# Attention's query projection moved behind the last value stream, and the latents' chunk matrices moved up behind the context's

## The chip, the cores and the metric

The kernel runs on one core of one Trainium2 chip. The metric is the device time of one execution in microseconds (us), the median of three runs. Inputs, weights and output are fp32 in the chip's memory; every projection reads its weights from there once.

## The reference, cut to what matters

The network has two layers on 256 latent tokens (and, in layer 0, 256 context tokens), width 2048. Layer 0 mixes tokens in two ways at once: eight heads of a bidirectional gated delta rule (GDN), and eight heads of attention. The change lies wholly in that mixer.

```python
def gated_delta_chunked(q, k, v, g, beta, s0):      # chunks of 64 tokens
    ...
    m = jnp.where(i[:, None] > i[None, :], jnp.einsum('bhnid,bhnjd->bhnij', kb, k) * decay, 0.0)
    t_inv = lax.linalg.triangular_solve(eye + m, ...)
    ...
    s_fin, o = lax.scan(step, s0, tuple(xs))         # state runs from chunk to chunk

def even_mixer(h, hc, ...):
    pc = hc @ w_in[:, ...]                           # context: keys and values alone
    o_c, s_ctx_fin = gdn_bidirectional(...)          # context first
    ka, va, kb, vb, a, b, qa, qb, za = split_segments(h @ w_in, EVEN_SEGS)
    ...
    o_l, _ = gdn_bidirectional(to_bhtd(q_l), ..., s_ctx_fin)   # latents start from the context's state
    y_gdn = gdn_out_norm(o_l, za, gdn_norm)
    y_na = neighbourhood_attention(heads(qb), heads(kb), heads(vb), k_ctx_na, v_ctx_na, rpb)
    y = jnp.concatenate([y_gdn, y_na], axis=-1) @ w_out
```

Behind the mixer come a SwiGLU feed-forward, layer 1 (a short convolution mixer) and a second feed-forward.

## The kernel before

**Projections.** A weight tile of 512 KB is loaded (`raw`, four rooms), split by ScalarE into a rounded half `whi` and by VectorE into the remainder `wlo` (L175, L246), and TensorE multiplies three products of halves (hi·hi, hi·lo, lo·hi). `fm_stream` (L344) gives features by tokens, `tm_stream` (L299, L300, L304 and, for the last weight tiles, L316) tokens by features; both yield once for each of 16 slices of the input width. The segments of `ev_w_in` are named KA, VA, QA (GDN's keys, values, queries), KB, VB, QB (attention's) and ZA (GDN's gate). QB is needed for the latents alone, so its matmuls are 256 columns wide; those of KB and VB are 512 wide.

**Side work.** `drive` runs a stream step by step. Where it is given `pump`, it lets so many adaLN jobs run for each step (`R_QB`, `R_KB`, `R_ZA`, `R_WO`): one job loads 256 KB of `ada_w` (`araw`) and adds a scaled copy to `acc` on VectorE (L434). Where `counts` is set, it counts steps and, at the steps in `P_INV`, runs the entries of `plan`.

**GDN.** `chunk_matrices(seq)` (seq 1 is the context, 0 the latents) builds the decayed key products `nt`, writes their parts out, and solves the 32 by 32 diagonal blocks by substitution on VectorE (62 small operations, L1018 and L1020). `inverses` assembles the inverse of four heads (a quad) from 32 to 128 by small matmuls on TensorE (L1074, L1081, L1087). `scan` runs the state over two chunks of two directions: for the latents each of the four rounds of a quad is a chain of L1112 and L1121 (state times keys, times queries), L1115 (`R`, VectorE), L1132 (inverse times `R`), L1136 and L1150 (ScalarE), L1140 and L1145 (the state's update) and L1154 (the output's second part).

**Attention.** For each head, `na_scores` loads the keys `kb`, the queries `qb` and a table of biases `bq` (L1289, rows of 256 bytes), adds the mask to the table on VectorE (L1292), multiplies (L1296, L1297) and takes the softmax (L1301 to L1305); `na_values` transposes the weights (L194) and multiplies by the values `vb` (L1320).

**Order in the program.** The context's chunk matrices are made first; QA and VA follow. Then come, counted as steps 1 to 96: two QB streams (32 steps; the result goes to `qb_d` in memory), KB, VB, KB, VB (64 steps; to `kb_d`, `vb_d`). At steps 30 and 32 the context's two quads are inverted; at step 32 the latents' chunk matrices and the context's scan follow; at steps 82 and 84 the latents' quads are inverted and scanned. After the streams come the eight heads of attention, ZA, the GDN heads' output norm, and the output projection W_out, whose first four slices are attention's heads 0 to 3 (`YO`).

This order is not what the engines run. A scheduler places each instruction by a simulated timeline, so work of neighbouring parts is interleaved on each engine's queue; each engine then runs its queue in that order. SyncE (SP) issues nearly all DMAs, one after the other, and an issue waits there until its buffer is free.

## Time and profile before

| | |
|---|---|
| runs | 2732.53 us median (2730.55 to 2732.67) |
| profiled execution | 2736.99 us |
| its span, first to last instruction | 2735.2 us |
| TensorE busy / VectorE / ScalarE / GpSimd | 97% / 70% / 47% / 2% of the span |
| mean granted TensorE clock | 0.991 |

A row of a window gives a stretch of the span, its length, then for each engine the busy time and the number of instructions in it, the granted TensorE clock as a share of full speed, the DMA engines' busy share and the rate in GB/s. PE is TensorE's matmuls, PEld its weight loads, DVE VectorE, ACT ScalarE, POOL GpSimd. A matmul of fp32 operands that were not rounded is two records. The records of matmuls overlap: one of 512 columns lasts about 0.39 us, and in a dense stretch the next starts after 0.23 us.

### The profile page before, as it was taken

To read this page: it belongs to the slowest core of one execution; us is meant where nothing else is said; L and a number is where in the kernel's file an instruction comes from. 1 tells how busy PE (TensorE), PEld (TensorE's weight loads), DVE (VectorE), ACT (ScalarE), POOL (GpSimd) and SP (SyncE) were. 2 spreads that over 40 slices of the span, in tenths; PEclk is the share of its full clock that TensorE was granted. 3 is DMA by queue.
4 is the path that set the end of the run, shared out by engine and by line. 5 is a ranking of instruction groups with operands and counts; after the bars stand their busy time and mean duration, and the time that the engine had idled before them with its cause. 6 is when DMAs were issued, how large, how long until landed. Compare 5 with 4: busy or idle time off the path is not lost.

```text
span 2735.2 us, 37578 instructions
## 1 busy us (share of the span) xinstructions
PE 2660.5 (97%) x13775; PEld 2188.8 (80%) x13775; DVE 1921.6 (70%) x2640; ACT 1276.9 (47%) x1849; POOL 56.7 (2%) x85
## 2 busy tenths in 40 slices
PE   6999999998989999999999999999999999999998
PEld 4688898886768888888888878888878888888886
DVE  4378796886658877766778878888575555545675
ACT  3257633323544544444455555444464444445554
POOL 0000100110000000000000000000000000000000
PEclk9999999998999999999999999999999999999999
DMA  9955598797737888888888859998567777656553
GB/s 368 347 156 181 167 315 259 271 342 216 234 108 258 290 287 293 299 292 277 291 284 288 297 157 336 324 337 280 184 225 235 226 238 226 219 188 220 195 194 112
DMA packets 286852, 684.80 MB, mean 250 GB/s; under 512 B 57161, under 2 KB 99761, under 8 KB 285259
## 3 DMA queue, kind: packets, MB, share of 16 engines
q1 hardware_dynamic: 280388, 669.26, 72.8%
q10 hardware_dynamic: 4375, 9.48, 1.0%
q0 software_dynamic: 1904, 3.67, 0.4%
q8 instruction: 108, 1.77, 0.2%
q14 instruction: 77, 0.63, 0.1%
HBM read 659.21 MB, written 23.10 MB: 249 GB/s over the span
## 4 chain that ended last, share of the span: by engine, by line
PE 88%; DMA 5%; DVE 3%; ACT 2%; SPq 1%; issue 1%; DVEq 0%; ACTq 0%
PE mm L299 21%; PE mm L304 21%; PE mm L300 21%; PE mm L344 10%; PE mm L316 8%; DMA araw<-in_ada_w_dram 2%; PE sm L194 2%; PE sm L595 1%; PE gd L344 1%; DMA bq<-in_ev_rpb_dram 1%; DMA raw<-in_ev_w_in_dram 1%; PE gd L938 1%; DVE wlo L246 0%; DMA xn<-in_ctx_dram 0%; SPq L1010 0%
## 5 line engine op out<-in xcount | busy, mean ns | idle before, releaser
L246 DVE TENSOR_TENSOR wlo<-raw,whi 128x1024 fp32r<-128x1024 f32 x800 | 971.9, 1222 | 457.9 <-ACT whi L175 444.4
L175 ACT ACTIVATE whi<-raw 128x1024 fp32r<-128x1024 f32 x800 | 843.5, 1062 | 886.8 <-PE mm L304 617.6
L299 PE MATMUL mm<-whi,fhi 128*128 128x512 f32 x1232 | 482.0, 393 | 2.6 <-DVE fhi L1437 2.6
L300 PE MATMUL mm<-wlo,fhi 128*128 128x512 f32 x1232 | 479.7, 390 | 0.5 <-DVE wlo L246 0.5
L304 PE MATMUL mm<-whi,flo 128*128 128x512 f32 x1232 | 389.9, 390 | 0.0
L399 DVE SCALAR_TENSOR_TENSOR acc<-araw,cT,acc 128x1024 f32<-128x1024 f32 x224 | 286.5, 1279 | 36.2 <-DMA araw<-in_ada_w_dram 32.9
L344 PE MATMUL mm<-hB,whi 128*128 128x512 f32 (+1 forms) x1064 | 273.5, 348 | 1.0 <-DVE hB L619 1.0
L299 PEld LDWEIGHTS mm<-whi,fhi 128*128 128x128 f32 x1232 | 231.3, 188 | 50.9 <-DVE fhi L1437 4.0
L304 PEld LDWEIGHTS mm<-whi,flo 128*128 128x128 f32 x1232 | 231.1, 188 | 48.4
L300 PEld LDWEIGHTS mm<-wlo,fhi 128*128 128x128 f32 x1232 | 231.2, 188 | 47.6 <-DVE wlo L246 1.2
L299 PE MATMUL mm<-whi,ahi 128*128 128x512 f32 x664 | 259.0, 390 | 0.0
L300 PE MATMUL mm<-wlo,ahi 128*128 128x512 f32 x664 | 258.3, 389 | 0.0
L304 PE MATMUL mm<-whi,alo 128*128 128x512 f32 x664 | 206.6, 389 | 0.0
L344 PEld LDWEIGHTS mm<-hB,whi 128*128 128x128 f32 x1064 | 181.4, 190 | 24.3 <-DVE hB L619 2.2
L344 PE MATMUL mm<-hB,wlo 128*128 128x512 f32 (+1 forms) x532 | 178.0, 347 | 0.6 <-DVE wlo L246 0.6
L434 DVE SCALAR_TENSOR_TENSOR acc<-araw,cT,acc 128x512 f32<-128x512 f32 x192 | 142.7, 746 | 24.8 <-DMA araw<-in_ada_w_dram 23.3
L178 ACT ACTIVATE ahi<-prodT 128x256 fp32r<-128x256 f32 x176 | 73.0, 418 | 182.9 <-PE mm L300 178.1
L304 PEld LDWEIGHTS mm<-whi,alo 128*128 128x128 f32 x664 | 124.6, 188 | 25.9
L300 PEld LDWEIGHTS mm<-wlo,ahi 128*128 128x128 f32 x664 | 124.7, 188 | 25.7
L299 PEld LDWEIGHTS mm<-whi,ahi 128*128 128x128 f32 x664 | 124.6, 188 | 25.7
L299 PE MATMUL mm<-whi,dhi 128*128 128x512 f32 x336 | 131.2, 393 | 1.2 <-DVE dhi L1437 1.2
L300 PE MATMUL mm<-wlo,dhi 128*128 128x512 f32 x336 | 130.8, 390 | 0.0
(410 smaller groups left out, 3413.9 us busy)
## 6 DMA issues: line engine op xcount, KB each, us to landing
araw<-in_ada_w_dram SPq DMA_DIRECT2D x288, 512.0 KB
raw<-in_ffn_w_down_dram SPq DMA_DIRECT2D x176, 512.0 KB
raw<-in_ffn_w_gate_dram SPq DMA_DIRECT2D x160, 512.0 KB
raw<-in_ffn_w_up_dram SPq DMA_DIRECT2D x160, 512.0 KB
raw<-in_ev_w_in_dram SPq DMA_DIRECT2D x112, 512.0 KB
araw<-in_ada_w_dram SPq DMA_DIRECT2D x192, 256.0 KB
raw<-in_od_w_in_dram SPq DMA_DIRECT2D x96, 512.0 KB
raw<-in_ev_w_out_dram SPq DMA_DIRECT2D x32, 512.0 KB
```

The lines of the kernel that those rows point to most:

```text
L175: ACT.activation(dst, src, AF.Copy)
L178: ACT.activation(hi, src, AF.Copy)
L194: return PE.transpose(dst, src, ident[:n, :n])
L246: last_lo[0] = DVE.tensor_tensor(lo, raw, hi, op=OP.subtract).ins
L299: PE.matmul(ps[ti][n], a, hi[:, n * 512:(n + 1) * 512], start=first, stop=False)
L300: ins = PE.matmul(ps[ti][n], a, lo[:, n * 512:(n + 1) * 512], start=False, stop=False).ins
L304: last_mm[0] = PE.matmul(ps[ti][n], b, hi[:, n * 512:(n + 1) * 512], start=False, stop=False).ins
L316: ins = PE.matmul(ps[ti][n], a(t), w[:, c_], start=False, stop=a is ll and hi is group[-1][0]).ins
L344: last_mm[0] = PE.matmul(o, wt, h_(slice(0, len(ws)), mv, k), start=i == 0 and g == 0 and j == 0, stop=i == len(ks) - 1 and g == len(group ...
L399: DVE.scalar_tensor_tensor(acc, raw, cT[:, k:k + 1], acc, op0=OP.mult, op1=OP.add)
L434: DVE.scalar_tensor_tensor(accs[n], raws.pop(i), cT[:, k:k + 1], accs[n], op0=OP.mult, op1=OP.add)
L595: ins = PE.matmul(pr[32 * j:32 * j + 32, :], cT2[:, g + j, :], raw[:, j].rearrange("p s n -> p (s n)"), start=g == 0, stop=g == KT - 4).ins
```

## The change

The two QB streams no longer come first. The first one, `queries(0)`, runs behind the last VB stream and ahead of attention's first scores; the second, `queries(1)`, inside the loop over heads, ahead of head 4's scores. Their results are not sent to memory: three pairs of heads stay in the staging rooms `nst`, the fourth in the room that `qb` had. The counted steps 1 to 64 are now KB, VB, KB, VB, and 65 to 96 the queries.

The latents' chunk matrices move from behind the context's second inverse (step 32) to step 2 (`P_CH`), ahead of both inverses of the context. So that both can be alive, the latents' `n64`, `n32`, `dgs` get rooms of other tiles (`o_t`, `vtok`), and the solve is done in place in `dgs`. The context's quads are inverted at steps 16 and 22, and the second quad's `xd` is loaded after the first inverse, into the same room; the latents' quads are inverted and scanned at steps 50 and 56. Loads of weights in attention, the queries and ZA are given high priority by the scheduler (`urgent`). The clearing of the mixer's `acc` goes from GpSimd to VectorE. Two pump rates change.

```diff
-P_INV = (30, 32, 82, 84)
+P_CH = 2
+P_INV = (16, 22, 50, 56)
...
-R_KB = 1.8
-R_ZA = 1.5
+R_KB = 1.6
+R_ZA = 2.0
...
-            SP.dma_start(raw[:, :, o:o + w], ap.rearrange("(k p) n -> p k n", p=128)[:, k0:k0 + nk, c0:c0 + w])
+            with tc.high_priority() if urgent[0] else Stack():
+                SP.dma_start(raw[:, :, o:o + w], ap.rearrange("(k p) n -> p k n", p=128)[:, k0:k0 + nk, c0:c0 + w])
...
-                POOL.memset(acc, 0.0)
+                DVE.memset(acc, 0.0)
...
+        else:
+            n64 = lgo.tile([128, 1024], F32, name="n64", tag="o_t", bufs=2).rearrange("p (n c) -> p n c", n=16)
+            n32 = g4("n32", "vtok")[:, 0:512].rearrange("p (n c) -> p n c", n=16)
+            dgs = lgo.tile([128, 1024], F32, name="dgs", tag="o_t", bufs=2)
...
-        zsol = g4("zsol", "diag").rearrange("p (r c) -> p r c", r=32)
+        zsol = g4("zsol", "diag") if seq else dgs.rearrange("p n c -> p (n c)")
...
+    def own_chunks():
+        nonlocal off, diag, own
+        own = chunk_matrices(0)
+        off = load_offdiag(parts)
+        diag = load_diag(parts[2], 0)
 
     def first_inverse():
-        xdTs.append(inverses(off, diag[0], 0))
+        nonlocal diag
+        xdTs.append(inverses(off, diag, 0))
+        diag = load_diag(parts[2], 1)
 
     def second_inverse():
-        nonlocal parts, off, diag
-        xdTs.append(inverses(off, diag[1], 1))
-        parts = chunk_matrices(0)
+        nonlocal off, diag
+        xdTs.append(inverses(off, diag, 1))
         for q in range(2):
             scan(q, 1, xdTs[q])
...
-    plan += [(P_INV[0], first_inverse), (P_INV[1], second_inverse), (P_INV[2], first_inverse), (P_INV[3], latents)]
+    plan += [(P_CH, own_chunks), (P_INV[0], first_inverse), (P_INV[1], second_inverse), (P_INV[2], first_own), (P_INV[3], latents)]
...
-    for q in range(2):
-        drive(fm_stream([(wv, C_QB + q * 512, 512)], ks, [0], stage_pairs(lambda f: qb_d[:, q * 4 + f:q * 4 + f + 2, :])), pump, R_QB, counts=True)
+    def queries(q):
+        drive(fm_stream([(wv, C_QB + q * 512, 512)], ks, [0], keep_pairs), pump, R_QB, counts=True)
...
-        qb = nap.tile([128, 256], F32, name="qb", tag="qb", bufs=2)
+        qb = pairs[h // 2][:, h % 2, :]
...
-        SP.dma_start(qb, qb_d[:, h, :])
...
+    urgent[0] = True
+    queries(0)
     held = na_scores(0)
     for h in range(8):
+        if h == 3:
+            queries(1)
         ahead = na_scores(h + 1) if h < 7 else None
         na_values(h, held)
         held = ahead
     drive(tm_stream([(wv, C_ZA, 1024)], ks, lhsh, [0, 1], za_evac), pump, R_ZA)
+    urgent[0] = False
```

What the scheduler makes of it is seen in the engines' queues. The first place is TensorE's queue at attention's first heads. Before, the work between the scores (`sm<-kb,qb` and the bias `sm<-bq,cs`) is the ZA stream (`mm<-whi,hC`):

```order
L299 MATMUL mm<-whi,hC 128x512 x4
L1296 MATMUL sm<-kb,qb 128x512 x2
L1297 MATMUL sm<-bq,cs 128x256 x2
L300 MATMUL mm<-wlo,hC 128x512 x2
L304 MATMUL mm<-whi,hC 128x512 x2
L1132 MATMUL gd<-R,xdT 128x128 x4
```

In the changed kernel (its line numbers are higher: 1313, 1314 for the scores, 348 for `fm_stream`, 1123 and 1143 for the scan) the work between the first heads is the queries' second stream, 256 columns wide, and the scores read `qst`, the pair on chip:

```order
L1143 MATMUL gd<-vtok,xdT 128x128 x4
L1313 MATMUL sm<-kb,qst 128x512
L1314 MATMUL sm<-bq,cs 128x256
L1313 MATMUL sm<-kb,qst 128x512
L1314 MATMUL sm<-bq,cs 128x256
L348 MATMUL mm<-hA,whi 128x256 x2
L348 MATMUL mm<-hA,wlo 128x256
```

So ZA is no longer used up beside the first heads; it follows them. The second place is TensorE's queue at the latents' scan. Before, its last rounds stand with nothing between their steps:

```order
L1112 MATMUL gd<-state,kT 128x128 x4
L1121 MATMUL gd<-state,qT 128x128 x4
L1132 MATMUL gd<-R,xdT 128x128 x4
L1154 MATMUL gd<-vn,AT 128x128 x4
L1112 MATMUL gd<-state,kT 128x128 x4
L1121 MATMUL gd<-state,qT 128x128 x4
L1132 MATMUL gd<-R,xdT 128x128 x4
L1140 MATMUL gd<-vd,ktok 128x128 x4
L1154 MATMUL gd<-vn,AT 128x128 x4
```

Before, 29 such rows of the scan stand from the last W_out rows of attention's heads on, with only transposes and heads' values between them. After, ZA's and W_out's rows (`mm<-whi,yhi`) stand between the steps of six rounds:

```order
L1165 MATMUL gd<-vn,AT 128x128 x4
L1123 MATMUL gd<-state,kT 128x128 x4
L1132 MATMUL gd<-state,qT 128x128 x4
L303 MATMUL mm<-whi,yhi 128x512 x4
L1143 MATMUL gd<-R,xdT 128x128 x4
L304 MATMUL mm<-wlo,yhi 128x512 x2
L308 MATMUL mm<-whi,ylo 128x512 x2
```

Only the last two rounds, eight rows, still stand bare ahead of the last two heads. The third place is SP's queue at the bias tables. Before, head 6's keys, queries and table:

```order
L232 DMA raw<-in_ev_w_out_dram 128x1024
L1290 DMA kb<-kb_d 128x512
L1291 DMA qb<-qb_d 128x256
L1289 DMA bq<-in_ev_rpb_dram 64x6x64 x2
L232 DMA raw<-in_ev_w_out_dram 128x1024 x3
```

After, the last head's (L1308 keys, L1307 table, L236 weights, L433 `ada_w`, L1328 values, L431 the bias row of `acc`):

```order
L236 DMA raw<-in_ev_w_in_dram 128x1024
L433 DMA araw<-in_ada_w_dram 128x512
L1328 DMA vb<-vb_d 128x4x128
L433 DMA araw<-in_ada_w_dram 128x512
L431 DMA acc<-in_ada_b_dram 1x512
L1308 DMA kb<-kb_d 128x512
L1307 DMA bq<-in_ev_rpb_dram 64x6x64 x2
```

The queries' loads are gone, weights of ZA stand where W_out's stood, and the table is issued behind weights and `ada_w` as before.

More of the change, by code (lines that the diff above doesn't have):

```diff
@@ L224, in rstd @@
         return r
+    urgent = [False]
     def load_w(segs, k0, nk):
@@ L956, in chunk_matrices @@
         t0 = 2 * seq
-        n64 = gw.tile([128, 16, 64], F32, name="n64", tag="n64", bufs=1)
-        n32 = gw.tile([128, 16, 32], F32, name="n32", tag="n32", bufs=1)
-        dgs = g4("dgs", "diag").rearrange("p (n c) -> p n c", n=32)
+        if seq:
+            n64 = gw.tile([128, 16, 64], F32, name="n64", tag="n64", bufs=1)
+            n32 = gw.tile([128, 16, 32], F32, name="n32", tag="n32", bufs=1)
+            dgs = g4("dgs", "diag")
+        else:
+            n64 = lgo.tile([128, 1024], F32, name="n64", tag="o_t", bufs=2).rearrange("p (n c) -> p n c", n=16)
+            n32 = g4("n32", "vtok")[:, 0:512].rearrange("p (n c) -> p n c", n=16)
+            dgs = lgo.tile([128, 1024], F32, name="dgs", tag="o_t", bufs=2)
+        dgs = dgs.rearrange("p (n c) -> p n c", n=32)
         for q in range(2):
@@ L1036, in load_offdiag, with load_diag @@
         return n64, n32
-    def load_diag(dz, q):
-        xd = g4("xd", "kT" if q else "diag").rearrange("p (n c) -> p n c", n=16)
+    def load_diag(dz, q, tag="diag"):
+        xd = g4("xd", tag).rearrange("p (n c) -> p n c", n=16)
         xdT = gw.tile([128, 16, 128], F32, name="xdT", tag="xdT", bufs=XDT)
@@ L1199, in body @@
     xdTs = []
-    off = load_offdiag(parts)
-    diag = [load_diag(parts[2], q) for q in range(2)]
+    off = diag = own = None
+    def own_chunks():
[3 more added lines that the diff above has]
+        diag = load_diag(parts[2], 0)
     def first_inverse():
-        xdTs.append(inverses(off, diag[0], 0))
+        nonlocal diag
+        xdTs.append(inverses(off, diag, 0))
+        diag = load_diag(parts[2], 1)
     def second_inverse():
-        nonlocal parts, off, diag
-        xdTs.append(inverses(off, diag[1], 1))
-        parts = chunk_matrices(0)
+        nonlocal off, diag
+        xdTs.append(inverses(off, diag, 1))
         for q in range(2):
@@ L1212, in second_inverse, with first_own @@
         xdTs.clear()
-        off = load_offdiag(parts)
-        diag = [load_diag(parts[2], q) for q in range(2)]
+        off = load_offdiag(own)
+        diag = [load_diag(own[2], q, ("diag", "kT")[q]) for q in range(2)]
+    def first_own():
+        xdTs.append(inverses(off, diag[0], 0))
     def latents():
@@ L1220, in body @@
     o_ts = []
-    plan += [(P_INV[0], first_inverse), (P_INV[1], second_inverse), (P_INV[2], first_inverse), (P_INV[3], latents)]
+    plan += [(P_CH, own_chunks), (P_INV[0], first_inverse), (P_INV[1], second_inverse), (P_INV[2], first_own), (P_INV[3], latents)]
     kb_d = dram.tile([128, 8, 512], F32, name="kb_d")
     vb_d = dram.tile([128, 4, 1024], F32, name="vb_d")
-    qb_d = dram.tile([128, 8, 256], F32, name="qb_d")
     def stage(dst):
@@ L1234, in stage, with keep_pairs @@
         return f
-    def stage_pairs(dst):
-        held = []
-        def f(i, p):
-            if not held:
-                held.append(nsp.tile([128, 512], F32, name="nst", tag="nst", bufs=NST).rearrange("p (f t) -> p f t", f=2))
-            ACT.activation(held[0][:, i % 2, :], p[:, 0:256], AF.Copy, scale=scale)
-            if i % 2:
-                SP.dma_start(dst(i - 1), held.pop())
-        return f
-    for q in range(2):
-        drive(fm_stream([(wv, C_QB + q * 512, 512)], ks, [0], stage_pairs(lambda f: qb_d[:, q * 4 + f:q * 4 + f + 2, :])), pump, R_QB, counts=True)
+    pairs = []
+    def keep_pairs(i, p):
+        if not i % 2:
+            t_ = (nsp.tile([128, 512], F32, name="qst", tag="nst", bufs=NST) if len(pairs) < NST else
+                  nap.tile([128, 512], F32, name="qb", tag="qb", bufs=1))
+            pairs.append(t_.rearrange("p (f t) -> p f t", f=2))
+        ACT.activation(pairs[-1][:, i % 2, :], p[:, 0:256], AF.Copy, scale=scale)
+    def queries(q):
+        drive(fm_stream([(wv, C_QB + q * 512, 512)], ks, [0], keep_pairs), pump, R_QB, counts=True)
     for q in range(2):
```

1 line of the change is left out of this document (added).

## The prediction

> **What bounds the kernel now.** I read the page first, then the windows (busy time by stretch), the chain that ended last, and the waits. The page says that TensorE is nearly always at work:
>
> ```profile
> PE 2660.5 (97%) x13775; PEld 2188.8 (80%) x13775; DVE 1921.6 (70%) x2640; ACT 1276.9 (47%) x1849; POOL 56.7 (2%) x85
> L246 DVE TENSOR_TENSOR wlo<-raw,whi 128x1024 fp32r<-128x1024 f32 x800 | 971.9, 1222 | 457.9 <-ACT whi L175 444.4
> L434 DVE SCALAR_TENSOR_TENSOR acc<-araw,cT,acc 128x512 f32<-128x512 f32 x192 | 142.7, 746 | 24.8 <-DMA araw<-in_ada_w_dram 23.3
> ```
>
> Busy hides something, since a matmul that runs alone is counted for its whole length. So I cut the mixer into stretches: the QB streams with KB and VB (320 to 606), ZA with attention (606 to 744), the latents' bare scan with the last heads (744 to 804), W_out (804 on), and take the number of matmuls in them.
>
> ```profile
> 320.00:606.00 286.00, 282.92 (x2041) 244.62 (x2040) 237.89 (x425) 97.46 (x151) 26.81 (x37) 1.00 0.87 287
> 606.00:744.00 138.00, 123.30 (x1040) 96.79 (x1039) 90.12 (x169) 62.04 (x123) 3.92 (x3) 0.93 0.80 244
> 744.00:804.00 60.00, 47.59 (x289) 40.88 (x287) 31.54 (x101) 26.73 (x93) 0.23 (x1) 0.89 0.11 35
> 804.00:890.00 86.00, 85.42 (x393) 70.23 (x392) 68.47 (x100) 36.41 (x52) 0.82 (x2) 1.00 0.78 270
> ...
> 606.00:804.00 198.00, 170.89 (x1326) 137.67 (x1324) 121.65 (x269) 88.77 (x216) 4.15 (x4) 0.91 0.59 180
> ```
>
> The granted clock is 1.00 wherever TensorE is fed without a pause and 0.93 and 0.89 in the two stretches between. What the matmuls of 606 to 804 need in a dense stream follows from the three windows by the tile written (`mm`, `gd`, `sm`) and from dense pieces of the chain and the timeline:
>
> ```profile
> 606.00:804.00 198.00, 63.72 (x238) 0.91 0.59 180
> 606.00:804.00 198.00, 72.38 (x912) 0.91 0.59 180
> 606.00:804.00 198.00, 46.34 (x176) 0.91 0.59 180
> 386.24 24.63 PE mm L344 x108
> 362.16 23.29 PE mm L344 x192
> 584.23 0.89 PE gd L1140 x8
> 699.82 1.10 PE gd L1074 x32
> 428.45 0.74 PE L1074 MATMUL gd<-xd,n 32*32 32x32 f32 x62
> ```
>
> A matmul of 512 columns takes 24.63 / 108 = 0.228 us, of 256 columns 23.29 / 192 = 0.121, of 128 columns 0.89 / 8 = 0.111; 32 of 64 by 64 take 1.10, some 64 of 32 by 32 about 0.7. So `mm` needs 238 x 0.228 = 54. `sm` (28 of 512, 84 of 256, 64 narrower) needs 24. `gd` needs 42.6 for 384 of 128 columns, 8.6 for the 512 small ones of four and six groups, and 2.3 for its 16 wider ones: 53. Together 131 of 198 us: **67 us are lost** there. Some 26 of them lie in 744 to 804 (60 less 29 groups of the scan at 0.89 and about 8 for the heads), 41 in 606 to 744.
>
> Why, the chain and the waits say. Until 744 it runs from landing to landing; behind that, from step to step of one scan:
>
> ```profile
> 639.40 9.44 DMA araw<-in_ada_w_dram
> 664.10 10.61 DMA raw<-in_ev_w_in_dram
> 685.14 8.24 DMA bq<-in_ev_rpb_dram
> 720.54 10.99 DMA bq<-in_ev_rpb_dram
> ...
> 780.45 0.91 PE gd L1112 x8
> 781.46 1.14 DVE R L1115 x4
> 782.63 1.17 PE gd L1132 x8
> 783.89 0.38 ACT vn L1150
> 784.31 1.28 PE gd L1154 x8
> 785.65 0.57 issue
> ```
>
> The last round takes 785.65 - 780.45 = 5.2 us, of which four groups of matmuls are 3.6. In the same 198 us VectorE stood still for these, and ScalarE for weights:
>
> ```profile
> DVE bq L1292 <- DMA bq<-in_ev_rpb_dram: 25.1, 7, 9.7
> DVE wlo L246 <- ACT whi L175: 10.5, 9, 3.6
> DVE o_t L1156 <- PE gd L1154: 10.4, 7, 3.0
> DVE state L1145 <- PE gd L1140: 8.2, 3, 4.7
> ...
> ACT whi L175 <- DMA raw<-in_ev_w_in_dram: 39.3, 8, 12.8
> ```
>
> VectorE is a strict queue: behind a bias table that has not landed stand the splits of ready weights, and TensorE runs dry behind them.
>
> **The change, part by part.** *The queries move.* Two streams of 192 matmuls at 0.121 us are 46.6 us of TensorE, and at their old place they take 335 to 385:
>
> ```profile
> 335.00:385.00 50.00, 46.47 (x383) 45.88 (x382) 1.00 0.84 288
> ```
>
> These 50 us leave the dense stretch; the 3.4 lost in them (0 to 3.4 regained: 3). In the attention stretch they fill. The work there becomes 131 + 47 = 178 us. If nothing of the 67 lost came back, the kernel would be shorter by 67.
>
> *What stays lost.* (a) The bare tail. Before, 29 rows of the scan stand bare, after 8, two rounds: of the 26 us lost about 11 belong to the last heads (785 to 804: 19 us, some 8 of work), which stay as they are, and 15 to the scan, of which 8/29 stay: 4. So 15 us, between 11 and 26. (b) The middle, 41 before. The tables still come late; 25.1 / 7 = 3.6 us per wait. One prepared weight tile of the queries is 24 x 0.121 = 2.9 us of matmuls, of ZA 24 x 0.228 = 5.5, and ZA is no longer spent on the first heads. So at least half of the tables' waits are covered: 12 us lost. The bounds are 0 (next to the nearest dense row below) and 41 (nothing covered). I stay near the lower, since VectorE's load there resembles that row: it gets 121.65 + 16 splits x 1.222 + 15 more jobs x 0.746 = 152 us of work for 178, 86%, and at 94% TensorE lost nothing in one stretch, 1.45 us of 20 in another, where DMA was full:
>
> ```profile
> 500.00:520.00 20.00, 20.00 (x112) 17.23 (x112) 18.83 (x35) 6.80 (x12) 3.40 (x5) 1.00 0.84 273
> 360.00:380.00 20.00, 18.55 (x155) 18.31 (x154) 18.44 (x29) 8.62 (x13) 1.81 (x1) 1.00 1.03 370
> ```
>
> *The earlier stretch gets denser.* 320 to 606 loses 50 us of time and 16 x 1.222 + 19 x 0.746 = 34 us of VectorE's work: 204 in 236, 86% instead of 83%. By the two rows above that costs between 0 and 236 / 20 x 1.45 = 17 us; I take 4, nearer to the first row, since DMA is at 0.87 there.
>
> *Clearing `acc` on VectorE.* Twelve clears at GpSimd's 526 ns (the nearest row) are 6.3 us of VectorE, half of them earlier than attention, inside the 86%: 0, between 0 and 6.
>
> ```profile
> L426 POOL MEMSET acc<- 128x512 f32 x12 | 6.3, 526 | 422.6 <-DVE o_t L1190 155.5 <-PE sm L441 133.7 <-PE sm L595 130.8
> ```
>
> *Nothing is paid or gained* for four stores and eight loads of queries: SP stands less than it issues there, but no step of the chain above is a query's landing. The kept pairs hold three staging rooms; behind that waits ZA's second half, one stream after heads 0 to 3 have been scored: 0. The context's second `xd` waits for the first inverse and its eight loads, about the 8.24 us of the table's landing; KB's and VB's matmuls lie beside it: 0, at most 10 if that cover fails. Queries read `hC` after 2.9 us instead of ZA's 5.5: 0 to 3. The latents' solve ends in VectorE's queue ahead of the context's scan, and no wait of the latents' inverses on it should show.
>
> The sum: -67 + 15 + 12 - 3 + 4 = **-39 us** on the profiled 2736.99. That execution lies 4.5 above the median of the runs, 2732.53; so 2693.5, say **2694**.
>
> *The clock.* At a mean clock of 0.91 over 198 us, up to 18 of the 67 are clock, not waiting, and it only falls where TensorE pauses. The Trainium skill, "TensorE: Matmul & The Clock Gate", section "What's actually happening", has the array's clock halved after an idle window of about 3.4 us and full again after a busy one. The windows above agree in sign (0.89 to 0.93 beside gaps, 1.00 elsewhere). By that rule, with the queries' matmuls between the waits, the clock's part goes entirely, as in the sum; if it did not, up to 16 us would stay and the sum would be -23.
>
> **The rivals.**
> *VectorE sets the pace.* All its waits come again on top of 152 us: 25.1 + 10.5 + 10.4 + 8.2 and some 11 of smaller ones are 65, so 217 us for 178 of matmuls: 39 lost instead of 27; with 17 in the earlier stretch the gain is 67 + 3 - 39 - 17 = 14: 2718. For it: one queue, 86% full. Against: at 94% it held elsewhere.
> *The order does not do what it says.* The tables' landings stay as late, the middle keeps its 41, the tail 15: -67 + 56 - 3 + 4 = -10: 2722. If the tail keeps its 26 too: no change, 2733. For it: SP issues each table behind weights as before, and two rounds of the scan stay bare.
> *Slower: every table fully late.* SP issues the table only when its room, three heads back, is free, and now behind ZA's and the queries' weights. If all eight stop VectorE for the longest landing, 10.99 us, and a weight tile covers 2.9 of it, TensorE loses 8 x 8.1 = 65; with the tail's 15 and 4 earlier that is 84 against 70: slower by 14, 2747. It decides where a head loses more than (70 - 19) / 8 = 6.4 us, a wait of 9.3; before, the mean was 3.6 and the longest 9.7.
> The Trainium skill, "DMA: Bandwidth & Descriptors", section "Queues, rings and completion order", says that each DMA engine takes descriptors in ring order, so early weights delay a table. One weight tile and one `ada_w` tile ahead of a table are 786 KB, 3.2 us at the 244 GB/s of the window; eight times that is 26 us, and the sum would be -13. The landings of 8 to 11 us above fit such queueing; but tiles stood ahead of the tables before too.
> *More:* all but the last heads' 11 is regained: -67 + 11 - 3 = -59: 2674.
>
> **Chances.** Forecast (28 to 50 saved) 0.56; VectorE or tables pacing (6 to 28 saved) 0.23; more than 50 saved 0.07; no change 0.07; slower 0.07. A measurement of this kernel can tell about 0.2%, 5.5 us, from no change. Faster is 0.56 + 0.23 + 0.07 = 0.86. The range leaves out the slower and unchanged cases and a part of "more", 0.2 at most: 2678 to 2724.
>
> **What would show it.** In the changed profile: 0.99 or more of granted clock across ZA and attention; a gap of 15 us or so between the last W_out slice of heads 0 to 3 and the next slice, instead of some 60; VectorE's wait for tables no longer than 25 us in total; no window of KB and VB below 19 of 20 us of matmuls. Wrong it is if VectorE's wait for the tables passes 50 us, if the context's inverses (L1074) show waits for `xd`, or if TensorE waits for queries' weights.

## The result, and the profile after

The changed kernel takes **2721.95 us** (median of 11 runs, 2717.24 to 2728.91) against 2735.91 (11 runs beside them): ratio **0.9957, 95% interval 0.9945 to 0.9968**, some 12 us saved where 39 were forecast (the ratio goes by the means of the runs, 2734.67 and 2722.82; the medians lie 14 apart). Its profiled execution took 2726.88 us, 10.1 less than the one of before and 4.9 above its own median.

Of the changed kernel, first TensorE's and its neighbours' line of the page:

```profile
PE 2655.1 (97%) x13775; PEld 2188.7 (80%) x13775; DVE 1923.7 (71%) x2652; ACT 1279.2 (47%) x1851; POOL 47.1 (2%) x73
```

then windows by stage: KB and VB (320 to 545), queries with attention and ZA (545 to 745), the scan's tail and the last heads (745 to 787), W_out (787 to 890):

```profile
320.00:545.00 225.00, 222.62 (x1547) 184.89 (x1546) 194.57 (x374) 75.87 (x116) 19.64 (x30) 0.99 0.85 275
545.00:745.00 200.00, 187.15 (x1637) 166.11 (x1636) 126.29 (x237) 86.86 (x181) 4.58 (x3) 0.97 0.73 221
745.00:787.00 42.00, 34.69 (x185) 28.39 (x183) 29.43 (x75) 27.02 (x75) 0.00 (x0) 0.92 0.39 137
787.00:890.00 103.00, 98.56 (x455) 81.51 (x453) 89.24 (x137) 43.11 (x67) 0.00 (x0) 0.97 0.78 280
```

The last window reaches some 10 us further into the program than the one of before that ends at 890 (455 matmuls, not 393). W_out's main part now starts at 787 instead of 804. The clock is 0.97 in the middle, not the 0.99 that the forecast asked for. Then the waits between 555 and 787, the total, the times and the longest:

```profile
DVE bq L1309 <- DMA bq<-in_ev_rpb_dram: 32.5, 8, 7.4
...
DVE wlo L250 <- ACT whi L176: 16.1, 12, 4.0
```

VectorE waits for the tables longer than before (25.1). And the chain of the changed kernel in the first queries stream, where the longest losses lie:

```profile
560.97 8.95 DMA bq<-in_ev_rpb_dram
570.48 1.22 DVE wlo L250
571.70 0.15 DVE acc L438
571.85 9.85 DMA vtok<-vd__151
...
594.97 0.86 PE sm L1313 x2
595.83 0.43 PE sm L1314 x2
```

The last two rows show an error of the forecast. An fp32 matmul that was not rounded is two records, and a record of 512 columns takes 0.86 / 2 = 0.43 us, of 256 columns 0.215, not the 0.228 and 0.121 of the rounded halves. With these, **lost time** is counted here as follows: for each matmul the time to the next one's start, less what its shape takes in a dense stretch (0.227, 0.12 and 0.111 us for 512, 256 and 128 columns; the two above for unrounded ones).

| stage | lost before | forecast after | lost after |
|---|---|---|---|
| streams ahead of attention | 8.0 | 1 more | 8.5 |
| attention's stretch | 28.8 (forecast: 41) | 12 | 21.5 |
| scan's tail and last heads | 23.4 (forecast: 26) | 15 | 12.6 |
| W_out | 1.7 | no more | 7.5 |
| sum | 61.9 | | 50.1 |

The stages are those of the windows, but W_out is counted to 880 in the changed kernel, where the same work ends as at 890 before. The difference is 11.8; ahead of 320 us the changed kernel loses 1.3 more, and its span is 10.1 shorter.

### The profile page after: what moved, and what is told of

It is laid out like the page before. It is cut to its first block, busy times and chain, and to the rows that moved or that the text cites. A ratio compares the mean times of both kernels' runs of the same rounds, so it can differ in the third digit from the quotient of the medians.

```text
span 2725.1 us, 37531 instructions
## 1 busy us (share of the span) xinstructions
PE 2655.1 (97%) x13775; PEld 2188.7 (80%) x13775; DVE 1923.7 (71%) x2652; ACT 1279.2 (47%) x1851; POOL 47.1 (2%) x73
## 4 chain that ended last, share of the span: by engine, by line
PE 91%; DMA 3%; DVE 2%; ACT 2%; issue 1%; SPq 1%; DVEq 0%; ACTq 0%
PE mm L303 22%; PE mm L308 21%; PE mm L304 21%; PE mm L348 10%; PE mm L320 8%; PE sm L195 2%; PE sm L599 1%; PE gd L348 1%; DMA bq<-in_ev_rpb_dram 1%; DMA araw<-in_ada_w_dram 1%; PE sm L1337 1%; PE gd L1143 0%; PE gd L942 0%; DMA xn<-in_ctx_dram 0%; DVE wlo L250 0%
## 5 line engine op out<-in xcount | busy, mean ns | idle before, releaser
L348 PE MATMUL mm<-hB,whi 128*128 128x512 f32 (+1 forms) x840 | 235.3, 366 | 1.0 <-DVE hB L623 1.0
L348 PEld LDWEIGHTS mm<-hB,whi 128*128 128x128 f32 x840 | 147.7, 189 | 24.3 <-DVE hB L623 2.2
L348 PE MATMUL mm<-hB,wlo 128*128 128x512 f32 (+1 forms) x420 | 149.5, 364 | 0.0
L303 PEld LDWEIGHTS mm<-whi,ahi 128*128 128x128 f32 x664 | 124.7, 188 | 25.7
L304 PEld LDWEIGHTS mm<-wlo,ahi 128*128 128x128 f32 x664 | 124.7, 188 | 25.5
```

The costliest lines, as they stand in the source:

```text
L303: PE.matmul(ps[ti][n], a, hi[:, n * 512:(n + 1) * 512], start=first, stop=False)
L304: ins = PE.matmul(ps[ti][n], a, lo[:, n * 512:(n + 1) * 512], start=False, stop=False).ins
L348: last_mm[0] = PE.matmul(o, wt, h_(slice(0, len(ws)), mv, k), start=i == 0 and g == 0 and j == 0, stop=i == len(ks) - 1 and g == len(group ...
```

## The experiments

Each ratio is to runs of the kernel before on the same chip; "lost" is counted as above between fixed times of each profile, and one execution can be off by some 5 us. In plain_tables, the two short_rows and before_odd the tables' values are left out; all others compute everything.

| kernel | median us | ratio to before, 95% interval | lost 320-550 | 550-745 | 745-895 |
|---|---|---|---|---|---|
| before | 2735.91 | 1 | 6.2 | 30.6 | 26.2 |
| changed | 2721.95 | 0.9957, 0.9945 to 0.9968 | 8.7 | 21.4 | 21.4 |
| queries_alone | 2741.33 | 1.0019, 1.0010 to 1.0029 | 13.1 | 25.5 | 27.7 |
| chunks_alone | 2727.63 | 0.9971, 0.9959 to 0.9982 | 8.3 | 27.1 | 17.7 |
| chunks_first | 2736.74 | 1.0003, 0.9992 to 1.0014 | 14.9 | 33.4 | 16.7 |
| tables_early | 2716.24 | 0.9930, 0.9918 to 0.9942 | 6.5 | 17.1 | 18.0 |
| mask_gpsimd | 2718.73 | 0.9937, 0.9925 to 0.9949 | 6.9 | 19.5 | 19.8 |
| acc_gpsimd | 2722.82 | 0.9952, 0.9939 to 0.9965 | 7.4 | 17.8 | 18.2 |
| vtok_room | 2731.88 | 0.9984, 0.9975 to 0.9993 | 8.9 | 25.7 | 21.3 |
| tables_and_vtok | 2721.37 | 0.9940, 0.9924 to 0.9956 | 7.7 | 19.4 | 20.0 |
| plain_tables | 2713.95 | 0.9926, 0.9910 to 0.9941 | 6.3 | 12.0 | 20.4 |
| tables_gpsimd_queue | 2723.51 | 0.9957, 0.9942 to 0.9973 | 6.3 | 17.5 | 24.5 |
| short_rows_even | 2711.20 | 0.9913, 0.9899 to 0.9926 | 7.2 | 9.1 | 19.7 |
| short_rows_odd | 2707.80 | 0.9905, 0.9891 to 0.9918 | 7.3 | 7.9 | 17.9 |
| before_odd | 2718.66 | 0.9935, 0.9921 to 0.9948 | 8.4 | 16.6 | 20.5 |
| tables_bounced | 2718.17 | 0.9943, 0.9928 to 0.9959 | 16.5 | 6.9 | 16.4 |
| bounced_late_mask | 2718.25 | 0.9941, 0.9927 to 0.9956 | 16.3 | 7.5 | 15.1 |
| bounced_spaced | 2735.51 | 0.9999, 0.9990 to 1.0008 | 29.7 | 8.7 | 20.6 |
| before_bounced | 2740.05 | 1.0012, 1.0003 to 1.0021 | 28.0 | 12.8 | 23.2 |
| tables_spread | 2714.68 | 0.9924, 0.9912 to 0.9936 | 8.4 | 7.7 | 20.7 |

### Which part of the change

**queries_alone**, from the changed kernel: `own_chunks` goes, its work returns into `second_inverse`.

```diff
-P_CH = 2
-P_INV = (16, 22, 50, 56)
+P_INV = (1, 2, 50, 52)
...
         xdTs.append(inverses(off, diag[1], 1))
+        parts = chunk_matrices(0)
...
```

> The queries' move alone: the changed kernel with the latents' chunk matrices back behind the context's second inverse (which now come at steps 1 and 2, as the queries no longer stand ahead of them); the latents' inverses at steps 50 and 52, so as many streams stand behind them as in the changed kernel, less two steps. Theory (the tail's gain of 12 us comes from the streams that now stand behind the latents' scan, whichever way the chunk matrices lie): within 4 us of 2722, the bare rounds of the scan as few as in the changed kernel. Rival (the early chunk matrices are what frees the latents' scan): 8 to 14 us slower than the changed kernel, no better than before.

It is slower than before, and the theory fell. The latents' solve, by its line's first and last start on VectorE, suggests why; in the kernel before, in the changed one, and in queries_alone:

```profile
L1018 DVE TENSOR_TENSOR sub_tmp<-lsol,zsol x31: 190/358/422, 562.8 to 614.2; 128x31 f32<-128x31 f32 x2, 128x60 f32<-128x60 f32 x2, 128x87 f32<-128x87 f32 x2, 128x112 f32<-128x112 f32 x2
```

```profile
L1029 DVE TENSOR_TENSOR sub_tmp<-lsol,dgs x31: 191/358/425, 494.2 to 546.9; 128x31 f32<-128x31 f32 x2, 128x60 f32<-128x60 f32 x2, 128x87 f32<-128x87 f32 x2, 128x112 f32<-128x112 f32 x2
```

```profile
L1021 DVE TENSOR_TENSOR sub_tmp<-lsol,zsol x31: 192/359/421, 567.4 to 651.8; 128x31 f32<-128x31 f32 x2, 128x60 f32<-128x60 f32 x2, 128x87 f32<-128x87 f32 x2, 128x112 f32<-128x112 f32 x2
```

Without the early chunk matrices the solve stands in the queries' and attention's stretch and ends at 652 instead of 547; the latents' scan starts at 718 instead of 657, and its rounds stand bare again (27.7 lost behind 745).

**chunks_alone**, from the kernel before: only the chunk matrices' move.

```diff
-P_INV = (30, 32, 82, 84)
+P_CH = 34
+P_INV = (48, 54, 82, 88)
...
```

> The chunk matrices' move alone, on the kernel before: the queries stay in front, go to memory and come back, and the old pump rates and GpSimd's clearing stay; the latents' chunk matrices come at step 34, the context's inverses at 48 and 54, the latents' at 82 and 88, which are the changed kernel's places counted with the 32 steps of the queries ahead. The queries' move alone came out 6 us slower than before. Theory (the two parts need each other: the early solve frees the latents' scan, the queries are the filler): 2 to 8 us faster than before, 2728 to 2734, the scan's tail partly bare. Rival one (the early chunk matrices are the whole gain): 10 us or more faster than before. Rival two (without the filler they only crowd the dense stretch): slower than before.

As the theory had it: 8 us faster, most of it behind 745 (26.2 to 17.7 lost). The parts alone give -8 and +5 (queries_alone keeps the change's pump rates, priorities and clearing), together -12: they need each other.

**chunks_first**: as chunks_alone, with `P_CH = 2` and `P_INV = (16, 22, 50, 56)`.

> As chunks_alone, but all of it 32 steps earlier, beside the queries in front: chunk matrices at step 2, the context's inverses at 16 and 22, the latents' at 50 and 56 of 96, so that as much work stands behind the latents' scan as in the changed kernel, without the queries being moved. Theory (what counts is how much work is left behind the start of the latents' scan): within 5 us of the changed kernel, 2717 to 2727, no bare rounds of the scan. Rival (attention's first heads need the queries' matmuls as a filler): no better than before by more than 5 us, with the tables' waits as large as before.

No better than before, as the rival had it, though not by its reason alone. The rounds are less bare (16.7 lost); 33.4 are lost beside attention's heads (30.6 before), but most is given back ahead of them, 14.9 instead of 6.2, and VectorE's waits for tables are shorter (18.4 us instead of 25.1). That the queries' matmuls are wanted beside the heads is not shown by this run. That the latents' scan started only at 695, in spite of its early step, I had not expected.

### Which wait of attention's stretch

**tables_early**, from the changed kernel (four rooms, loads a head early, the mask behind the last head's scaling):

```diff
-        DVE.tensor_tensor(bq, bq, bandf[:, None, :].to_broadcast([128, 6, 64]), op=OP.add)
+        with tc.issue_after(last_s[0] or last_lo[0]):
+            DVE.tensor_tensor(bq, bq, bandf[:, None, :].to_broadcast([128, 6, 64]), op=OP.add)
...
+    for h in range(4):
+        table(h)
     urgent[0] = True
     queries(0)
...
```

> Of the changed kernel this moves only the bias tables: a fourth room for `bq`, the first four tables are loaded ahead of the queries and each later one a head earlier, and the mask is added on VectorE only behind the last scaling of the head before, so that the table has landed by then. Theory (landings of tables stop VectorE's queue, and TensorE runs dry behind it): VectorE's wait for tables, 32.5 us in the changed kernel, falls under 8, TensorE's loss between 545 and 660 us (19 us there) falls to under 8, and the time falls by 10 to 15 us, to about 2710. Rival (VectorE's load sets the pace, and the tables' waits only stand where it would be late anyway): the wait falls too, but weights' remainders and softmax steps are late instead, and the time stays within 4 us of 2722.

VectorE's wait for tables is gone from the view, but only 5.7 us came back and 14.8 are still lost from 550 to 660. With the tables out of VectorE's way the chain of this kernel names another landing at the same place, for which TensorE waits 6.5 us:

```profile
567.14 7.95 DMA vtok<-vd__151
575.13 2.08 PE gd L1143 x8
```

**mask_gpsimd**, from the changed kernel: `POOL.tensor_tensor(bq, bq, ...)` instead of `DVE.tensor_tensor`.

> Of the changed kernel this moves only the mask's addition to the table (8 of 128 x 384) from VectorE to GpSimd; the loads stay where they are. Theory (the harm is that VectorE's queue stands behind a landing): splits go on while a table is on its way, and 8 to 15 us go, to 2707 to 2714. Rival one (scores need the table anyway and stand in TensorE's own queue): TensorE waits for the table at the bias matmul instead, and the time stays within 4 us of 2722. Rival two (GpSimd's addition slows VectorE beside it): slower than 2724.

3 us came back, with intervals that overlap: less than the theory asked for. TensorE does not wait for the tables at the bias, as rival one had it, but 8.4 us for the same `vtok`. VectorE's standing still is a part of the harm only.

**acc_gpsimd**, from the changed kernel: `POOL.memset(acc, 0.0)` instead of `DVE.memset(acc, 0.0)`.

> Of the changed kernel this undoes one line: `acc` is cleared on GpSimd again instead of VectorE. Theory (the clears cost nothing where they stand): within 3 us of 2722. Rival (SP stood 27.4 us on VectorE's clearing of `acc` ahead of W_out, and loads behind it came late): 3 to 6 us faster than the changed kernel, and the loss of 8.6 us in W_out's stretch (787 to 890) falls to about 3 as before the change.

The theory held: no cost of the clears shows. W_out's loss, 5.5 between the same matmuls instead of 7.5, does not bear the rival out either.

**vtok_room**, from the changed kernel: the second `vtok` of the context in a room of its own.

```diff
-        vtok = load_tok("vtok", vd_, 2 * seq, q)
+        vtok = load_tok("vtok", vd_, 2 * seq, q, seq and q)
...
-        t = g4(tag, tag).rearrange("p (t h e) -> p t h e", t=2, h=4)
+        t = lgo.tile([128, 1024], F32, name=tag, tag="o_t", bufs=2) if own else g4(tag, tag)
...
```

> Of the changed kernel this gives one load another room: the values `vtok` of the context's second quad go to a free `o_t` room, so that SP issues them right behind the first quad's instead of behind the first quad's last read. Theory (a landing of `vtok` that takes 9.85 us in the chain stops TensorE's queue at 565 to 582 us, in the middle of the first queries stream): TensorE's loss of 10 us between 550 and 600 falls to under 4 and the time falls by 5 to 8 us, to about 2716. Rival (the stretch is short of weights, and whatever stands first in the queue takes the blame): the loss stays, with weights or tables as the owner, and the time stays within 3 us of 2722.

The theory fell: `vtok` is no longer late, 9.4 us are still lost from 550 to 600, now behind tables, and the whole is 10 us slower than the changed kernel. The latents' inverses and scan come later (scan from 669 instead of 657); why it is as much as 10 us is not settled.

**tables_and_vtok**: both edits.

> The early tables with their late mask (as in tables_early) and the room for the context's second `vtok` together. Theory (two separate landings on two queues): the gains add, 5.5 and 5 to 8 us, to about 2710. Rival (one stretch, one loss): what the second takes away is already gone, and the time stays within 3 us of 2716.

Nothing adds up: at 2721 it is neither the theory's 2710 nor the rival's 2716. It looked like one stretch with one loss, whichever landing stands first in a queue, and so like a cause common to all landings.

### What in a table's load

In the changed kernel, the DMA view of 562 to 568 us, and the window of its last table, where TensorE ran on:

```profile
DMA packets 859, 0.42 MB, mean 70 GB/s; under 512 B 750, under 2 KB 750, under 8 KB 858
```

```profile
668.00:674.00 6.00, 6.00 (x40) 5.42 (x39) 1.16 (x4) 2.42 (x4) 0.00 (x0) 1.00 0.46 69
```

A table's 768 packets of 256 bytes take 4 to 8 us. From 562 to 568 70 GB/s is all that moves, their own bytes included, though a weight tile, keys and `ada_w` were issued behind. From 668 to 674 nothing was left to hold up: SP issued the next weight tile at 675.7, and 69 GB/s is what a table alone makes of its time. Where two tables follow each other beside weights (570.8 to 585.6 and 602 to 614.4), 240 and 218 GB/s pass: the engines are slowed, not always stopped. Of the measurements below, plain_tables and the two short_rows change only the tables' source, tables_gpsimd_queue only their queue.

**plain_tables**

```diff
-            src = bass.AP(tensor=ev_rpb.tensor, offset=ev_rpb.offset + h * 465 + (5 - half) * 31 + 15 - 63,
-                          ap=[[1, 64], [31, 6], [1, 64]])
+            src = ada_w[0][h * 128 + half * 64:h * 128 + half * 64 + 64, 0:384].rearrange("p (s c) -> p s c", s=6)
```

> A measurement: of the changed kernel only the source of the eight bias tables is another, 64 rows of 1536 bytes in a row of another input instead of 64 x 6 overlapping rows of 256 bytes; the table's values, and with them attention's biases, are left out. In the changed kernel's trace each table is some 750 packets of 256 bytes, and for 5 to 6 us the DMA engines move little else (70 GB/s from 562 to 568, 80 from 650 to 655, 69 from 668 to 674). Theory (a table's transfer holds up everything issued behind it, weights too, so the short queries tiles run out): VectorE's wait for tables falls from 32.5 to under 10 us, TensorE's loss from 550 to 660 (19 us) to under 8, the time by 10 us or more, to 2712 or less, below tables_early's 2716. Rival one (only VectorE's queue standing behind the table matters): the same as tables_early, 2716. Rival two (the stretch is short of weights whatever the tables do): within 3 us of 2722.

8 us came back. The interval overlaps that of tables_early almost wholly, so this run doesn't tell the theory from rival one; 9.4 were still lost from 550 to 660, and VectorE still waited 12.3 for tables. The scheduler also placed TensorE's instructions in another order here (724 of 13775 places).

**tables_gpsimd_queue**, from the changed kernel: `POOL.dma_start` for the tables instead of `SP.dma_start`.

> Of the changed kernel only the queue of the eight tables' loads is another: GpSimd issues them instead of SP. Theory (the harm is order: weights that SP issued behind a table wait for it): weights pass the table, TensorE's loss from 550 to 660 falls by 5 us or more, 2717 or less, though the tables themselves land no sooner. Rival (the 256-byte packets hold the 16 engines themselves, whichever queue they come from): within 3 us of 2722, and the rate in the tables' stretches stays near 70 to 110 GB/s.

The rival held: the same time as the changed kernel. The DMA view of 567 to 569, with the tables on GpSimd's queue:

```profile
DMA packets 56, 0.10 MB, mean 48 GB/s; under 512 B 13, under 2 KB 13, under 8 KB 56
```

Weights from SP's queue crawl all the same: a tile that SP issued at 565.4 had landed for ScalarE only at 574.0. So a table's place in SP's queue is not the cause. (A table's packets are recorded as 2 to 4 KB on this queue, so it isn't their number either; and the order of TensorE's instructions differs from the changed kernel's.)

**short_rows_even** and **short_rows_odd** put one of these in the place of the two removed lines above:

```diff
+            src = bass.AP(tensor=ada_w.tensor, offset=ada_w.offset + (h * 2 + half) * 64 * 4096,
+                          ap=[[4096, 64], [512, 6], [1, 64]])
...
+            src = bass.AP(tensor=ada_w.tensor, offset=ada_w.offset + (h * 2 + half) * 64 * 4097,
+                          ap=[[4097, 64], [512 + 31, 6], [1, 64]])
```

> A measurement: of the changed kernel only the source of the eight bias tables is another: again 64 x 6 rows of 256 bytes for each half, but apart from each other and each on a multiple of 2 KB in another input; the table's values are left out. Theory (short rows as such are slow): each table still takes 5 us or more at about 130 to 150 packets per us, and the time is that of the changed kernel within 3 us, 2722. Rival (it is where the rows lie, over each other in 2 KB or off any boundary): a table's 768 packets pass in 2 us or less, as the 2048 packets of 128 bytes of `xd` did in about 2 us, and the time is that of plain_tables within 3 us, 2714.

> A measurement: as short_rows_even, with the rows still apart from each other, but each partition's rows shifted by 4 bytes more than the last one's, so that almost none lies on a boundary; the table's values are left out. If addresses off a boundary are what is slow, a table takes 5 us or more as in the changed kernel, and the time is near 2722; if it is that the rows lie over each other in 2 KB, it takes 2 us or less and the time is near 2714.

Both ways the gather is quick, and these are the fastest of all runs, 2711 and 2708. TensorE's instructions stand in the changed kernel's order, in short_rows_odd but for two, so nothing but the source differs. The DMA view of short_rows_odd, 560 to 562:

```profile
DMA packets 805, 0.26 MB, mean 131 GB/s; under 512 B 777, under 2 KB 777, under 8 KB 804
```

777 short packets in 2 us, where the overlapping rows needed 6 us for 750. Short rows are not what is slow, nor rows off a boundary; it is that the 384 rows of each half **lie over each other** within (63 + 5 x 31 + 64) x 4 bytes, some 1.1 KB. (Whether the overlap does it or the one small place, tables_spread tells in part.) With that gone, attention's stretch is nearly dense. Its window in short_rows_odd:

```profile
540.00:725.00 185.00, 182.41 (x1637) 162.32 (x1636) 126.34 (x239) 85.15 (x176) 6.26 (x5) 1.00 0.75 240
```

The same 1637 matmuls as in the changed kernel's 200 us stand in 185, at a clock of 1.00, 6.0 lost by the count above.

**before_odd**: the kernel before with short_rows_odd's source.

> A measurement: the kernel before with the tables' source of short_rows_odd (rows apart from each other, off boundaries; the values are left out) and nothing else changed. short_rows_odd was 14 us faster than the changed kernel. Theory (before, ZA's tiles of 5.5 us covered more of a table's 5 to 6 us than the queries' 2.9, but the tables were in the same 41 us of the forecast): 6 to 12 us faster than before, 2724 to 2730; the change then brings some 18 us once tables are harmless, against 13 with them. Rival one (the harm is the same in both kernels): 14 us or more faster, 2722 or less, and the change is worth the same 13. Rival two (before, the tables were covered): within 4 us of before, and the change's full worth is 27 us.

The first rival held: 17 us faster than before, against 14 (2721.95 - 2707.80) for the changed kernel. The tables cost both kernels nearly the same; the queries' matmuls took 3 off it. Without the tables' harm the change is worth 2718.66 - 2707.80 = 11 us, or 8 by the two ratios. TensorE's order is the one of before, so its middle can be set beside the 138 us from 606 to 744:

```profile
609.70:726.90 117.20, 113.19 (x1039) 91.13 (x1038) 90.91 (x169) 62.55 (x123) 3.72 (x3) 1.00 0.88 284
```

By the count above 7.8 us are lost in it, where before lost 28.8.

### Cures

**tables_bounced**, from the changed kernel, **bounced_late_mask** (with tables_early's mask) and **bounced_spaced** (gathers by SP, one for seven steps):

```diff
+    def table_out(h):
+        st_ = nsp.tile([128, 512], F32, name="bst", tag="nst", bufs=NST)[:, 0:384].rearrange("p (s c) -> p s c", s=6)
+        ...
+            POOL.dma_start(st_[half * 64:half * 64 + 64], src)
+        POOL.dma_start(bq_d[:, h], st_)
...
+        SP.dma_start(bq, bq_d[:, h])
```

> Of the changed kernel: the eight tables are gathered early, in the first KB and VB streams, by GpSimd's queue into a staging room and stored to memory as rows of 1536 bytes; attention loads them from there. The mask is added where it was. Theory (the gather's packets are harmless where a weight tile lasts 5.5 us of TensorE and four are ahead): VectorE's wait for tables under 12 us, no stretch of under 120 GB/s between 560 and 680, 8 to 14 us faster than the changed kernel, 2708 to 2714. Rival (the gather costs as much where it is put): TensorE loses 5 us or more in 320 to 480 instead, and the time stays within 4 us of 2722.

> As tables_bounced, and the mask is added on VectorE only behind the last scaling of the head before, with each table loaded a head early as in tables_early (three rooms). Theory (two harms, the packets and the queue behind a landing): 2 to 5 us faster than tables_bounced, about 2706, the fastest of all runs. Rival (a quick landing leaves nothing for the late mask to win): within 2 us of tables_bounced.

> As tables_bounced, but the eight gathers are issued by SP and spread over the KB and VB streams, one for seven steps, each behind a weight's split in the order; GpSimd only stores them. In tables_bounced the loss from 550 to 660 fell from 19 to 4.4 us, and 7.8 us were given back before 550, in two places where two gathers stood together or beside other loads (5.5 us at 428, 3.5 at 498). Theory (the gather is harmless where a weight tile lasts 5.5 us, if one stands alone): the loss from 550 to 660 stays near 4.4 us, the one from 320 to 550 falls back to about 9, and the time is 2708 to 2713, the fastest of all runs that compute everything. Rival (a gather costs 1 us or more wherever it stands): 2716 to 2719, as tables_bounced.

**before_bounced**: the kernel before with the spread gathers.

> The kernel before, with the same spread gathers as bounced_spaced and nothing else changed. Theory (in the kernel before the tables also stop VectorE for 25 us and hold up weights, beside ZA's longer tiles): 4 to 10 us faster than before, 2725 to 2731, with the scan's bare tail left; then the change brings 14 us or more on top of it, which is more than it brings without. Rival one (the tables' loss and the change's gain are the same time): 12 us or more faster than before. Rival two (ZA's tiles covered the tables already): within 3 us of before.

All four take attention's loss away (6.9 to 8.7 in the changed kernel's, 12.8 in before's) and give it back ahead of it. So tables_bounced missed its theory, and its rival held. The late mask adds nothing once landings are quick, its rival's case. bounced_spaced and before_bounced came out slower than theory and rivals alike, the latter slower than before. bounced_spaced gave back most: its GpSimd queue stood behind the landings, and copies of the chunk matrices stood in that queue; that this is the reason is argued from its waits, not tested. Its waits between 320 and 560:

```profile
POOL bq_d L1255 <- DMA bst<-in_ev_rpb_dram: 69.5, 7, 25.4
...
PE gd L942 <- DVE nt L987: 6.7, 2, 3.7
```

**tables_spread**: one copy of the bias array for each partition.

```diff
+    rpb_d = dram.tile([64, 3784], F32, name="rpb_d")
+    with tc.issue_after(last_lo[0]):
+        POOL.dma_start(rpb_d[:, 0:3720], bass.AP(tensor=ev_rpb.tensor, offset=ev_rpb.offset, ap=[[0, 64], [1, 3720]]))
...
+                          ap=[[3785, 64], [31, 6], [1, 64]])
```

> The changed kernel with the cure that short_rows_odd points to, and everything computed: ahead of the KB streams GpSimd's queue copies the whole bias array (14.9 KB) 64 times into memory, one copy for each partition, and the tables' rows are read each from its partition's own copy. Theory (it is the rows lying over each other that is slow): a table's packets pass in 2 to 3 us, the loss from 550 to 660 falls from 19 to 5 us or less, the copying (1 MB) costs under 3 us beside the dense stretch, and the time is 2708 to 2713, the fastest of all kernels that compute everything. Rival (the 64 copies, read from one place, hold the engines as the tables did, or the gather is slow again): 2717 or more.

Of the kernels that compute everything it has the fastest median, 7 us below the changed kernel: ratio 0.9924 (0.9912 to 0.9936), an interval below that of the changed kernel; tables_early's overlaps it. The time lies between theory and rival. From 550 to 660 5.4 us are lost instead of 19. The six rows of a partition still overlap here (64 elements every 31), and yet a table passes as quickly as in short_rows_odd; so it is the rows of 64 partitions in one small place that are slow, not overlap as such. And the 64 copies, all read from the same 14.9 KB, passed with 276 GB/s moved in all (2 to 6 us): large packets from one place were not slow. It stays 7 us above short_rows_odd by the medians, 5 by the ratios: the copy was issued at 1.3 us, in the kernel's first, DMA-bound stretch. The window of 40 to 70 us, in tables_spread and in short_rows_odd:

```profile
40.00:70.00 30.00, 25.88 (x140) 15.43 (x141) 8.67 (x26) 5.22 (x9) 0.00 (x0) 0.94 1.08 374
```

```profile
40.00:70.00 30.00, 28.04 (x150) 17.29 (x151) 8.51 (x24) 5.27 (x10) 0.00 (x0) 0.94 1.09 377
```

Ten matmuls are missing, and the 50th to the 700th of the projections' come 3.3 us later all along. A copy issued later, between 100 and 300 us, where DMA is at 0.5 to 0.7, wasn't tried.

## Why the prediction was wrong

The direction and the tail were right, the size was not: 12 us instead of 39. The time lies within the range, close to the slow end to which the rivals had stretched it.

- **The tail: right.** 23.4 lost became 12.6, where 26 were to become 15. The last heads keep 9 of it. That the early chunk matrices earn this, not the streams behind the scan alone, queries_alone showed.
- **The streams ahead: right.** 0.5 more instead of 4 - 3 = 1.
- **"67 us are lost": mis-sized by 15.** `sm` was counted at the rate of rounded halves; by the chain's rows 52 were lost. Most of the excess, 12, stood in the middle's 41.
- **The failed step is "(b) The middle": "So at least half of the tables' waits are covered: 12 us lost."** Of 28.8 lost, 21.5 stayed. With a harmless source and the same order of TensorE's work 7.8 are lost before and 6.0 after. So in these profiles the tables made 21 of the middle's loss before and 15.5 after (by the medians 17 and 14): a quarter was covered, not half. Two things stand against the cover. VectorE's queue is one: from 562.7 to 570.0 VectorE waits for a table, and behind that wait stand the remainders of two tiles that had landed and whose rounded halves ScalarE had finished at 563.1 and 564.4. In the changed kernel, ScalarE, VectorE and TensorE:

```profile
563.32 1.06 ACT L176 ACTIVATE whi<-raw 128x1024 fp32r<-128x1024 f32 x1 [0.21 <-PE mm L348]
570.01 0.56 DVE L1309 TENSOR_TENSOR bq<-bq,cs 128x384 f32<-128x384 f32 x1 [7.33 <-DMA bq<-in_ev_rpb_dram]
570.48 1.22 DVE L250 TENSOR_TENSOR wlo<-raw,whi 128x1024 fp32r<-128x1024 f32 x1
571.76 0.39 PE L348 MATMUL mm<-hC,wlo 128*128 128x256 f32 x1 [4.36 <-DVE wlo L250]
```

  The filler was there and couldn't be used. The other is the DMA engines, through which the filler's weights come as well: `vtok` took 9.85 us beside the tables, and a weight tile issued at 576.3 let ScalarE wait 6.2 us, until 584.3. Taking the tables out of VectorE's way (mask_gpsimd, and tables_early, which also loads them earlier) gave back 3 to 6 of the 14 us; how the rest divides isn't shown.
- **W_out: a term that was left out, 6 us.** The forecast gave the 15 additional `ada_w` jobs to attention's stretch. In the trace they stand in W_out: 48 jobs there (787 to 890) in the changed kernel, 32 before (804 to 890). By their lines in these windows, and TensorE's timeline at the last of them:

```profile
L438 DVE SCALAR_TENSOR_TENSOR acc<-araw,cT,acc x48: 623/746/754, 796.8 to 868.2; 128x512 f32<-128x512 f32 x48
```

```profile
L434 DVE SCALAR_TENSOR_TENSOR acc<-araw,cT,acc x32: 740/745/754, 813.0 to 862.3; 128x512 f32<-128x512 f32 x32
```

```profile
865.41 0.39 PE L320 MATMUL mm<-whi,ylo 128*128 128x512 f32 x1
869.03 1.87 PE L445 MATMUL sm<-cs,acc 128*128 128x1 f32 x8 [3.24 <-DVE acc L438]
```

TensorE waits for the sum of the last job. Between the same matmuls 5.5 to 7.7 us are lost in all 15 kernels with the change's pump rates, which have 48 jobs there, and at most 1.8 in the five with the old rates, which have 32. But these five also have the queries in front, and a run with other rates alone wasn't made, so the cause is argued, not shown.

Together these are 12 (size) + 9.5 (21.5 instead of 12) + 5.8 (7.5 instead of 1.7) = 27.3; the stages missed the forecast by 39 - 11.8 = 27.2.

**The clock:** 0.97 in the changed kernel's middle, 1.00 in short_rows_odd's, where TensorE hardly pauses; the clock follows the waits. It is granted by halves, for 3.4 us at a time: 0.50 from 572.0 to 575.4, behind the pause of 4.4 us, and again from 582.2 to 585.7, behind one of 2.0. The Trainium skill's rule ("TensorE: Matmul & The Clock Gate", "What's actually happening") agrees in the halving and the length, but the trace shows that a pause shorter than its idle window was enough the second time. **The rivals:** VectorE did not set the pace; with 126 us of work in short_rows_odd's 185 TensorE lost only 6.0. The ring order of the Trainium skill ("DMA: Bandwidth & Descriptors", "Queues, rings and completion order") gave -13, close to the result, but weights ahead of a table in its queue are not what makes the harm: on another queue the tables did the same. The second rival, with tables as late as before and the tail alone regained, is nearest to what happened; that its 2722 is the measured time is partly luck, since 7 us of the middle did come back and W_out, which it left out, took 6.

**What would show it.** VectorE's wait for tables was to stay under 25 us and took 32.5; the gap behind the last W_out slice of heads 0 to 3 was to be 15 us and was 30.6 (70.5 before); and TensorE waited once, 4.4 us, for the remainder of the queries' weights, a sign named as one of being wrong. All three spoke against the forecast. KB's and VB's windows of 20 us held 18.9 us of matmuls or more, by and large as forecast, and no wait of the context's inverses for `xd` shows on TensorE.

## What to carry to other kernels

Before matmuls are moved to cover a late load, look at which queue stands behind that load, and whether it is the one that prepares the filler; and at what the DMA engines move meanwhile: if the rate falls there, the filler's own weights can be late too. A gather of many short rows out of one small place is worth spreading, by one copy for each partition; here the copy cost 3.3 us where DMA was full. Side work that is paced by steps has to be counted up to its last job: what the moved stretch doesn't take stands at the end, ahead of whoever needs the sum.

## What the hardware showed that I had not expected

- 768 rows of 256 bytes, 384 of them within 1.1 KB at a time, took 4 to 5 us with little beside them (54 to 116 GB/s in all, the changed kernel at 630, 650 and 669 us) and up to 8 beside weights; as many rows apart from each other, on or off a boundary, took 1.5 to 2, up to 4.8 beside weights. Rows that overlap only within a partition (tables_spread) are as quick. What in the memory makes it so stays open.
- The hold does not depend on the queue: with GpSimd as issuer 48 GB/s passed from 567 to 569.
- An unrounded fp32 matmul takes 0.43 us a record at 512 columns and 0.215 at 256, near twice a rounded half's.
